# An encoder step on one core: plain tiles in two single accumulation banks, up inputs scaled once, memory keys moved ahead

## The chip, the core and the metric

One core of a Trainium2 chip runs one layer of an encoder. The metric is the device time of one execution, in microseconds (us). The engines of the core are called TensorE (PE, matmuls), VectorE (DVE), ScalarE (ACT), GpSimd (POOL) and SyncE (SP, which here issues DMAs).

## What is computed

```python
# x: 512 prompt + 64 sample tokens, D_MODEL = 1024; mem: 256 tokens; all float32
x += MixerBlock(RMSNorm(x))      # gated DeltaNet || gated linear attention, sigmoid-gated merge,
                                 # then the output projection (wo)
x += MemCrossAttn(RMSNorm(x), mem)   # 4 heads of 256: mq, mk, mv, softmax, mo
x += ConvFFN(RMSNorm(x))         # up (2 x 2816), causal conv of width 3, SiLU gate, down
y = RMSNorm(x)                   # outputs: y, the memory keys and values, and the new states
```

## The kernel before

Activations lie with features on partitions, eight tiles of 128, and tokens along the free axis: 576 columns, which the FFN pads to 580. Every float32 operand is split into a high and a low part (tiles with names in h and l, such as `xh` and `xl`, `oh` and `ol`, `ach` and `acl`), and a product is three matmuls: high weight by high and by low, low weight by high. Each runs as two matmuls over the columns, 256 and 320, or 290 and 290 in the FFN. So a *plain tile* (128 output features, eight tiles of input) is 48 matmuls. Where two output tiles share inputs, `products` (L1523) and `up_product` (L1953) work a pair with seven products of sums instead of eight: 84 matmuls for 96. These sums of weights (`ws`) and of activations (`ce`, `co`, `tu`, `tw`, `sh`, `sl`, `sw`) are made by VectorE, ScalarE and GpSimd.

PE accumulates in eight banks: `big` (L500) hands out two tiles of two banks each, `sm` (L503) four single banks. Plain tiles take `big`; products, norms, the attention and the recurrences take `sm`. A tile is emptied (evacuated) into SBUF in two pieces, 512 prompt and 64 sample columns (`pv`, `two`), before its buffer goes on. Weights come as raw tiles (`wr`), from which ScalarE casts the high half and VectorE subtracts the low half, or by DMAs that add into a tile (`w<-wt`, `w<-ws`); nine weight tiles exist. `fetch` (L638) brings weights ahead as far as tiles are free and `wlimit` allows.

The program's order is not written out. A `Driver` (L225) keeps a clock of its own for each engine: it walks the main chain, which yields time as it places matmuls, and lets spawned chains (`c_...` functions) place their work when their inputs are ready by its cost model. `V`, `A`, `G` name VectorE, ScalarE, GpSimd; `X` picks whichever ends sooner; `together` places several instructions as one piece, back to back. Because every instruction is written by one helper, the profile gives all of them line L257, and tiles tell them apart.

The stages that the change touches, in order:
- *Output tiles* (`out_tile`, L1754), eight rows m of two plain tiles each (one per branch), multiplied into the gates `gt` by VectorE. After rows 0 to 3 stand the gates' products, whose operands a chain makes from gate row 2 on (`GT0`).
- *The list* `ATT` (L115): the order of memory keys (`mk`), memory values (`mv`), the output projection (`wo`, by products, over the stored input `x`) and the queries (`mq`), one step per head. `c_norm` makes the queries' inputs behind `wo`.
- *Memory output* (`mo`): tiles 0 and 1 are plain and wait for the last head, and are ended by `mo_last` (L1915); tiles 2 to 7 are products (`MPAIRS`). Tile 0 is ended ahead of the products, tile 1 after. As each x tile ends, `c_mo` (L1860) adds its square to `acc` and makes the up inputs `xh` (ScalarE, x by gain, 512 and 64 columns) and `xl` (VectorE); `c_sums` (L1879) adds them back to `ce` and `co` and makes the sums of the FFN's products from them.
- *The up loop* (L2057): up tiles 0 to JS - 1, each in a pair j and 22 + j, are plain; the first takes its inputs in the order 0, 2, 3, 4, 5, 6, 7, 1. `up_evac` (L1945) multiplies the tile by the norm's broadcast `rbc`, so the first pair waits for the norm n3. The other pairs are products.
- *The down projection*: three parts as plain tiles (`dn1`, L2075) between the products, the rest by products.

Of the kernel before, what the change touches and what calls it, by code (L numbers as in the profile page):

```python
# [30 lines left out]
WF = 3  # L31
RF = 1
NGDN = 2
GT0 = 2
HOP = 0.2
BACK = 6.0
MARGIN = 0.6
# [74 lines left out]

WPAIRS = [(("wo", m), ("wo", m + 1)) for m in range(0, 8, 2)]

ATT = [("mk", 0), ("mv", 0), ("wo", 0), ("mv", 1), ("mk", 1), ("mq", 0), ("mq", 1), ("mk", 2), ("mq", 2), ("mk", 3), ("mq", 3)]  # L115
MPAIRS = [(("mo", m), ("mo", m + 1)) for m in range(2, 8, 2)]
JS = 5
AFTER = {8: 2, 9: 2, 10: 2, 11: 2, 14: 2, 15: 2, 16: 2, 17: 2, 20: 2, 21: 2}


# [338 lines left out]
def tile_trunk(ctx, tc, xT, memT, wt, wd, vec, cst, w0, wgate, st_gdn, st_conv, st_gla, st_ffn, ckT, cv,  # L459
# [43 lines left out]
    def sm():  # L503
        return drv.rotate("sm", 4, pq.tile([P, 512], F32, tag="sm", name=nm("sm")))

    def r4(ap, b=128):
        return ap.rearrange("p (a b) -> p a b", b=b)

# [61 lines left out]
    def emit_product(pair, prod):  # L570

        def dram(tile_):
            kind, idx = tile_
            if kind != "dn":
                return wt[WIDX[tile_]], 512
            m, p = idx
            n = len(PARTS[p]) * 64
            return wd[m, :, PART0[p] * 128:PART0[p] * 128 + 2 * n], n

        n = dram(pair[0])[1]  # L580
        if prod == "P1":
            r = halves_of[pair] = []
            for t_ in pair:
                raw = raw_tile()
                src, _ = dram(t_)
                DMA(raw[:, :2 * n], src)
                r += [(raw[:, 0:n], src[:, 0:n]), (raw[:, n:2 * n], src[:, n:2 * n])]
        r = halves_of[pair]
        (a11, d11), (a12, d12), (a21, _), (a22, d22) = r[:4]

        def total(a, b):
            s_ = slot("ws")
            V.tensor_tensor(s_[:, 0:n], a, b, op=ALU.add)
# [151 lines left out]
    def two(t_, o1=0, o2=TP):  # L745
        return r4(t_[:, o1:o1 + TP], 256), t_[:, o2:o2 + TS]

    def tile_proj(kind, idx, xs, box, order=None, w=T):
        wh, wl = weight(kind, idx)
        ps = big()  # L750
        box.append(ps)
        yield from proj(ps, wh, wl, xs, late=kind in SUMMED, order=order, w=w)

# [808 lines left out]
    def main():  # L1562
# [191 lines left out]
        def out_tile(m):  # L1754
            wh, wl = weight("out", m)
            gs = [gates.pop((kd, m)) for kd in ("gta", "gtb")]
            for a in range(2):
                ps = big()
# [58 lines left out]
        for kd, i in ATT:  # L1817
# [10 lines left out]
            else:  # L1828
# [20 lines left out]
        acc = slot("acc")  # L1849
        out = []  # L1850
        yield tuple(("att", hd) for hd in range(3))
        part = []
        for m in range(2):
# [5 lines left out]
        yield (("att", 3),)  # L1859
        def c_mo(m):  # L1860
            yield [x[m]]
            sq_acc(acc, x[m], m == 0)
            h, lo = slot("xh", F32R), slot("xl", F32R)
            g = vcol(C_GFFN + m)
            for t_ in (h, lo):
                G.memset(pads(f(t_)), 0.0)
# [3 lines left out]
            out.append((m, (h, lo)))  # L1870
            drv.done.add(("mo", m))
            fx[m] = h, lo
            if m ^ 1 in fx:
                drv.spawn(c_sums(m // 2))

# [2 lines left out]

        def c_sums(k):  # L1879

            (eh, el), (oh_, ol_) = fx[2 * k], fx[2 * k + 1]
            ce, co = slot("ce"), slot("co")
# [32 lines left out]
        def mo_last(m):  # L1915
            ps, wh, wl = part[m]
            yield from proj(ps, wh, wl, xs_of(ao[6:8]), False, True, k0=6)
            for xx, i in zip(two(x[m]), pv(ps)):
                V.tensor_tensor(xx, i, xx, op=ALU.add)
# [9 lines left out]
        wlimit[0] = len(WORDER)  # L1929
        out = [p for _, p in sorted(out, key=lambda t: t[0])]  # L1930
        xs = xs_of(out, 580)
# [12 lines left out]

        def up_evac(col, ps):  # L1945
            u = up_tile()
            V.tensor_tensor(r4(u[:, 2:582], 290), ps[:, :, 0:290], r4(N["rbc"][:, 0:580], 290), op=ALU.mult)
            states(col, u)
            return u

        ubanks, fus = {}, {}
# [105 lines left out]
        for kd, i in FFN[:-1]:  # L2057
            if kd == "up":
                j = i
                ba_, bb_ = [], []  # L2060
                yield from tile_proj("up", j, xs, ba_, (0, 2, 3, 4, 5, 6, 7, 1) if j == 0 else None, 580)
                if j == 0:
                    yield from tile_proj("up", NJ, xs, bb_, None, 580)
                    yield ("n3",)
                    use_norm("n3")
                drv.spawn(c_gate(j, up_evac(j, ba_[0])), 1)
                if j > 0:
                    yield from tile_proj("up", NJ + j, xs, bb_, None, 580)
# [6 lines left out]
            elif kd == "dn1":  # L2075
                m, p = i
                yield tuple(("act", j) for j in PARTS[p])
                wh, wl = weight("dn", i)
                ps = big()
                yield from proj(ps, wh, wl, act_of(p), late=True)  # L2080
                for xx, i_ in zip(two(x[m]), pv(ps)):
                    V.tensor_tensor(xx, xx, i_, op=ALU.add)
                if m == 7:
                    for k in PARTK[p]:
                        del full[k]
# [296 lines left out]
```

## Time and profile before

| | us |
|---|---|
| median of 3 runs | 1115.37 (1115.36 to 1116.72) |
| the profiled execution | 1116.34 |
| its span | 1114.6 |
| PE busy | 1092.0 |
| VectorE, ScalarE, GpSimd busy | 744.1, 692.8, 316.1 |

All times are counted from the start of the span. "Busy" is the time in which an engine works on an instruction; of PE it says nothing on the clock, which the throttle can halve: the profile has the granted clock as a column of its own, 1.00 being full speed. In a row of waits, `PE big L257 <- DVE gt` says that PE, about to write a tile `big`, was released by VectorE's instruction that writes `gt`. In a timeline row stand start, length, engine, operation, output and inputs, shape and count, and in brackets the idle time before it with what ended it. The DMA share is that of the sixteen DMA engines.

### The profile page before, as it was taken

How to read it: one execution, taken by the hardware profiler on the slowest of the kernel's cores; microseconds unless marked ns; L12 is line 12 of the kernel's file. 1: busy time of each engine (PE TensorE's matmuls, PEld its weight loads, DVE VectorE, ACT ScalarE, POOL GpSimd, SP SyncE). 2: the span in 40 equal slices, each digit the busy share in tenths (PEclk: the TensorE clock that was granted, in tenths of full speed). 3: DMA queues.
4: the chain of work that ended last, by engine and by line, in shares of the span. 5: the costliest groups of instructions: out<-in, count | busy, mean ns of one | idle time of the engine just before them, and what ended most of it. 6: DMA issues, size and time to landing. Idle time of an engine off the chain costs nothing. (4 is left out here: it accounts for less than half of the span.)

```text
span 1114.6 us, 21435 instructions
## 1 busy us (share of the span) xinstructions
PE 1092.0 (98%) x8227; PEld 1053.9 (95%) x8227; DVE 744.1 (67%) x1466; ACT 692.8 (62%) x1360; POOL 316.1 (28%) x549
## 2 busy tenths in 40 slices
PE   9999999999999999998999999999999999999997
PEld 8999989998988999898999999899999999999996
DVE  5666854864654866876557579657776777577665
ACT  6666646563754577475647666665875785668644
POOL 0344215230432222131210124223432333334321
PEclk9999999999999999999999999899999999999999
DMA  8666532454455779596764737775887887788744
GB/s 284 135 161 144 116 74 78 81 116 111 124 108 120 175 175 229 162 273 180 191 177 110 188 71 167 189 170 111 176 178 163 188 185 172 157 200 184 169 99 117
DMA packets 66598, 173.04 MB, mean 155 GB/s; under 512 B 7744, under 2 KB 14016, under 8 KB 66496
## 3 DMA queue, kind: packets, MB, share of 16 engines
q0 software_dynamic: 29808, 72.89, 38.1%
q1 hardware_dynamic: 36400, 98.26, 27.1%
q8 instruction: 65, 1.06, 0.4%
q10 hardware_dynamic: 288, 0.52, 0.1%
q14 instruction: 37, 0.30, 0.1%
HBM read 158.94 MB, written 5.37 MB: 147 GB/s over the span
## 5 line engine op out<-in xcount | busy, mean ns | idle before, releaser
L257 PE MATMUL big<-xh,w 128*128 128x256 f32 (+1 forms) x1728 | 322.3, 304 | 3.3 <-ACT xh L257 2.2
L257 PEld LDWEIGHTS big<-xh,w 128*128 128x128 f32 x1728 | 261.2, 191 | 8.7 <-POOL xl L257 2.4
L257 POOL DMA_DIRECT2D w<-wt x146 | 129.4, 893 | 364.8 <-ACT w L257 281.6
L257 PE MATMUL big<-xl,w 128*128 128x256 f32 (+1 forms) x864 | 185.9, 297 | 0.0
L257 ACT CAST w<-wr 128x512 fp32r<-128x512 f32 (+3 forms) x200 | 158.6, 796 | 23.2 <-PE big L257 17.3
L257 ACT ACTIVATE w<-wr 128x512 fp32r<-128x512 f32 (+3 forms) x179 | 142.5, 798 | 28.7 <-PE big L257 7.5
L257 PEld LDWEIGHTS big<-xl,w 128*128 128x128 f32 x864 | 144.8, 190 | 0.2 <-DVE xl L257 0.2
L257 PE MATMUL sm<-xh,w 128*128 128x290 f32 (+1 forms) x640 | 137.6, 297 | 0.3 <-DMA w<-wt 0.3
L257 PE MATMUL sm<-ach,w 128*128 128x288 f32 (+2 forms) x576 | 119.9, 299 | 6.0 <-DVE x L257 2.7
L257 PE MATMUL big<-ach,w 128*128 128x256 f32 (+1 forms) x672 | 119.6, 295 | 0.5 <-ACT ach L257 0.5
L257 PEld LDWEIGHTS sm<-xh,w 128*128 128x128 f32 x640 | 106.3, 189 | 0.5 <-DMA w<-wt 0.5
L257 PEld LDWEIGHTS big<-ach,w 128*128 128x128 f32 x672 | 101.7, 188 | 0.8 <-ACT ach L257 0.7
L257 PEld LDWEIGHTS sm<-ach,w 128*128 128x128 f32 x576 | 94.7, 190 | 7.6 <-DMA w<-ws 2.3
L257 ACT CAST w<-ws 128x512 fp32r<-128x512 f32 (+1 forms) x120 | 70.7, 602 | 33.9 <-DVE ws L257 17.3
L257 PE MATMUL sm<-xl,w 128*128 128x290 f32 (+1 forms) x320 | 87.9, 296 | 0.0
L257 PE MATMUL sm<-acl,w 128*128 128x288 f32 (+2 forms) x288 | 79.5, 297 | 0.0
L257 DVE SCALAR_TENSOR_TENSOR fc<-fu,vec,fc 128x578 f32<-128x578 f32 x88 | 71.3, 825 | 8.3 <-ACT fc L257 7.8
L257 PE MATMUL big<-acl,w 128*128 128x256 f32 x336 | 71.9, 295 | 0.3 <-DVE acl L257 0.3
L257 DVE TENSOR_TENSOR w<-ws,w 128x512 fp32r<-128x512 f32 (+1 forms) x91 | 61.2, 682 | 8.3 <-ACT w L257 6.6
L257 PEld LDWEIGHTS sm<-xl,w 128*128 128x128 f32 x320 | 60.5, 189 | 0.0
L257 PE MATMUL sm<-sh,w 128*128 128x290 f32 x272 | 57.8, 298 | 1.0 <-DMA w<-ws 1.0
L257 PEld LDWEIGHTS big<-acl,w 128*128 128x128 f32 x336 | 56.2, 188 | 0.5 <-DVE acl L257 0.5
(390 smaller groups left out, 2190.0 us busy)
## 6 DMA issues: line engine op xcount, KB each, us to landing
wr<-wt SPq DMA_DIRECT2D x134, 512.0 KB, 5.7
w<-wt POOLq DMA_DIRECT2D x62, 512.0 KB, 7.1
w<-wt POOLq DMA_DIRECT2D x84, 256.0 KB, 6.1
wr<-wd SPq DMA_DIRECT2D x24, 384.0 KB, 6.7
w<-wd POOLq DMA_DIRECT2D x24, 384.0 KB, 6.9
w<-ws POOLq DMA_DIRECT2D x28, 256.0 KB, 5.9
x<-xT SPq DMA_DIRECT2D x16, 288.0 KB, 5.6
mem<-memT SPq DMA_DIRECT2D x8, 256.0 KB, 4.8
```

Source lines behind the costliest of these rows:

```text
L257: fn(*args, **kw)
```

## The change

A plain tile of the output rows, the up loop and `dn1` now takes either a two-bank tile or a pair of single banks (`wide`): the single ones if two of the four come free over 0.3 us earlier, on the Driver's clock. Its evacuation follows the banks (256 and 320 columns, or 512 and 64), both pieces placed as one. Memory keys 1 and 2 stand ahead of the output projection. `c_mo` scales x once into `cx` (ScalarE, two instructions placed as one), casts `cx` to `xh` (ScalarE, 580 columns) and subtracts for `xl` (VectorE), and `c_sums` uses `cx` itself. The first up tile takes its inputs in the order 2, 3, 4, 5, 0, 6 (high weight by high and low), the low weight by the same six, and then 7 and 1, with a wait of its own for each input; the first up pair is copied out by ScalarE as it is and scaled later. The norm n3 is started by a chain of its own. One weight more may be fetched before the memory output ends, and the gate operands start one gate row later. One more up pair goes by products. The sums of weights of `wo` and `mo` go to VectorE or GpSimd, whichever ends sooner.

```diff
-GT0 = 2
+GT0 = 3
-ATT = [("mk", 0), ("mv", 0), ("wo", 0), ("mv", 1), ("mk", 1), ("mq", 0), ("mq", 1), ("mk", 2), ("mq", 2), ("mk", 3), ("mq", 3)]
+ATT = [("mk", 0), ("mv", 0), ("mk", 1), ("mk", 2), ("wo", 0), ("mv", 1), ("mq", 0), ("mq", 1), ("mq", 2), ("mk", 3), ("mq", 3)]
-JS = 5
+JS = 4
+    def wide():
+        q = sorted(max([0.0] + list(drv.wrote.get(n, {}).values()) + list(drv.seen.get(n, {}).values())) if n not in drv.fresh else float("inf")
+                   for n in drv.ring["sm"])
+        if len(q) == 4 and q[1] + 0.3 < drv.free_at("big")[0]:
+            return Pair(sm(), sm())
+        return big()
...
         def total(a, b):
-            V.tensor_tensor(s_[:, 0:n], a, b, op=ALU.add)
+            (X if pair[0][0] in ("wo", "mo") else V).tensor_tensor(s_[:, 0:n], a, b, op=ALU.add)
...
         def out_tile(m):
-                ps = big()
+                ps = wide()
-                for g, i in zip(two(gs[a]), pv(ps)):
-                    V.scalar_tensor_tensor(g, g, 1.0, i, op0=ALU.add, op1=ALU.mult)
+                V.together([("scalar_tensor_tensor", (g, g, 1.0, i), dict(op0=ALU.add, op1=ALU.mult)) for i, g in pieces(ps, gs[a])])
...
         def c_mo(m):
-            for a, b, n in ((0, 0, TP), (TP + 2, TP, TS)):
-                A.activation(h[:, a:a + n], x[m][:, b:b + n], AF.Identity, scale=g)
-                V.scalar_tensor_tensor(lo[:, a:a + n], x[m][:, b:b + n], g, f(h[:, a:a + n]), op0=ALU.mult, op1=ALU.subtract)
+            A.together([("activation", (c_[:, a], x[m][:, b], AF.Identity), dict(scale=g))
+                        for a, b in ((slice(0, TP), slice(0, TP)), (slice(TP + 2, TP + 2 + TS), slice(TP, T)))])
+            parts2(h[:, 0:580], lo[:, 0:580], c_[:, 0:580])
...
         def c_sums(k):
-            for c_, (h, lo) in ((ce, (eh, el)), (co, (oh_, ol_))):
-                X.tensor_tensor(c_[:, 0:580], f(h)[:, 0:580], f(lo)[:, 0:580], op=ALU.add)
+            (eh, el, ce), (oh_, ol_, co) = fx[2 * k], fx[2 * k + 1]
...
-        wlimit[0] = WORDER.index(("up", 0)) + 1
+        wlimit[0] = WORDER.index(("up", 0)) + 2
-        yield tuple(("mo", m) for m in range(8))
-        drv.spawn(c_rstat("n3", [(acc, 0)], 4, True, 2.0, None, TP + 2))
+        def first_up(ps):
+            wh, wl = weight("up", 0)
+            outs = [(ps[:, 0, 0:290], U1), (ps[:, 1, 0:290], U2)]
+            for ks in ((2, 3, 4, 5, 0, 6), (7, 1)):
+                for k in ks:
+                    yield (("mo", k),)
+                    h, lo, _ = fx[k]
+                    for o, c in outs:
+                        PE.matmul(o, wh[:, k * 128:k * 128 + 128], h[:, c], start=k == 2, stop=False)
+                    for o, c in outs:
+                        PE.matmul(o, wh[:, k * 128:k * 128 + 128], lo[:, c], start=False, stop=False)
+                    yield 0.7
+                for k in ks:
+                    for o, c in outs:
+                        PE.matmul(o, wl[:, k * 128:k * 128 + 128], fx[k][0][:, c], start=False, stop=k == 1)
+                    yield 0.4
+            wlimit[0] = len(WORDER)
...
+        def raw_evac(ps):
+            u = up_tile()
+            A.together([("copy", (u[:, 2 + c:292 + c], ps[:, i, 0:290]), {}) for i, c in ((0, 0), (1, 290))])
+            return u
...
                 if j == 0:
-                    yield from tile_proj("up", NJ, xs, bb_, None, 580)
+                    yield from tile_proj("up", NJ, xs, bb_, None, 580, wide)
+                    u0, u1 = raw_evac(ba_[0]), raw_evac(bb_[0])
                     yield ("n3",)
```

The change moves instructions. First VectorE, at output rows 6 and 7 before: `big_5535` and `big_5576` are row 6's tiles, `gt_5105` and `gt_5106` its gates, the 1024-column rows the low halves of weights of memory key 0.

```order
L257 SCALAR_TENSOR_TENSOR gt_5105<-gt_5105,big_5535 128x64
L257 TENSOR_TENSOR w_5453<-wr_5451,w_5452 128x1024
L257 SCALAR_TENSOR_TENSOR gt_5106<-gt_5106,big_5576 128x64
L257 TENSOR_TENSOR w_5534<-wr_5532,w_5533 128x1024
L257 SCALAR_TENSOR_TENSOR gt_5105<-gt_5105,big_5535 128x512
L257 SCALAR_TENSOR_TENSOR ml_5587<-mem_5378,vec,mh_5586 128x256 x2
L257 SCALAR_TENSOR_TENSOR tw_5575<-tu_5574,gt_4854 128x288
L257 SCALAR_TENSOR_TENSOR ml_5605<-mem_5379,vec,mh_5604 128x256 x2
L257 SCALAR_TENSOR_TENSOR gt_5106<-gt_5106,big_5576 128x512
```

The same place now, where row 6 is in `big_5544` and `big_5586`, and row 7's first tile in `sm_5625` and `sm_5626`:

```order
L257 TENSOR_TENSOR w_5457<-wr_5455,w_5456 128x1024
L257 TENSOR_TENSOR w_5543<-wr_5541,w_5542 128x1024
L257 SCALAR_TENSOR_TENSOR ml_5585<-mem_5382,vec,mh_5584 128x256
L257 SCALAR_TENSOR_TENSOR gt_5113<-gt_5113,big_5544 128x512
L257 SCALAR_TENSOR_TENSOR gt_5113<-gt_5113,big_5544 128x64
L257 TENSOR_TENSOR tu_5594<-gt_4973,gt_4857 128x288
...
L257 SCALAR_TENSOR_TENSOR gt_5114<-gt_5114,big_5586 128x512
L257 SCALAR_TENSOR_TENSOR gt_5114<-gt_5114,big_5586 128x64
...
L257 SCALAR_TENSOR_TENSOR gt_5246<-gt_5246,sm_5625 128x256
L257 SCALAR_TENSOR_TENSOR gt_5246<-gt_5246,sm_5626 128x320
```

The two pieces of a tile stand together, and row 7 no longer uses the two-bank tiles. Second ScalarE, at the end of the memory output before; `x_5780` is tile 1, the last, and the 1024-column rows are casts of up weights:

```order
L257 ACTIVATE sq_8470<-x_5780 128x576
L257 ACTIVATE xh_8471<-x_5780,vec 128x512
L257 ACTIVATE w_8476<-wr_8474 128x1024
L257 CAST w_8475<-wr_8474 128x1024
L257 ACTIVATE w_8479<-wr_8477 128x1024
L257 ACTIVATE xh_8471<-x_5780,vec 128x64
L257 CAST w_8478<-wr_8477 128x1024
```

And now, with `x_5767` as tile 1:

```order
L257 ACTIVATE sq_8527<-x_5767 128x576
L257 ACTIVATE cx_8530<-x_5767,vec 128x512
L257 ACTIVATE cx_8530<-x_5767,vec 128x64
L257 CAST xh_8528<-cx_8530 128x580
L257 CAST sh_8563<-tu_8510 128x580
L257 CAST sw_8581<-tw_8511 128x290
L257 ACTIVATE w_8590<-wr_8588 128x1024
```

The input's rows stand together ahead of the weights. Third VectorE at the same place before, from the evacuation of tile 1 on:

```order
L257 TENSOR_TENSOR x_5780<-big_7837,x_5780 128x512
L257 TENSOR_TENSOR x_5780<-big_7837,x_5780 128x64
L257 SCALAR_TENSOR_TENSOR xl_8466<-x_6181,vec,xh_8465 128x512
L257 SCALAR_TENSOR_TENSOR xl_8466<-x_6181,vec,xh_8465 128x64
L257 TENSOR_TENSOR ce_8467<-xh_8439,xl_8440 128x580
L257 TENSOR_TENSOR co_8468<-xh_8465,xl_8466 128x580
L257 SCALAR_TENSOR_TENSOR tw_8434<-tw_8434,co_8390 128x290
L257 TENSOR_TENSOR sw_8469<-tw_8434,sw_8469 128x290
L257 TENSOR_TENSOR acc_7726<-acc_7726,sq_8470 128x576
L257 SCALAR_TENSOR_TENSOR xl_8472<-x_5780,vec,xh_8471 128x512
```

And now, to the low half of tile 1 (`xl_8529`):

```order
L257 TENSOR_TENSOR x_5767<-big_7850,x_5767 128x512
L257 TENSOR_TENSOR x_5767<-big_7850,x_5767 128x64
L257 TENSOR_TENSOR xl_8456<-cx_8457,xh_8455 128x580
L257 TENSOR_TENSOR sw_8473<-tw_8413,sw_8473 128x290
L257 TENSOR_TENSOR tu_8510<-cx_8457,cx_8444 128x290
L257 TENSOR_TENSOR acc_7753<-acc_7753,sq_8527 128x576
L257 SCALAR_TENSOR_TENSOR tw_8511<-tu_8510,cx_8444 128x290
L257 TENSOR_TENSOR xl_8529<-cx_8530,xh_8528 128x580
```

The two sums `ce` and `co` are gone, and the low halves are one row each.

More of the change, by code (lines that the diff above doesn't have):

```diff
@@ L504, in sm, with __init__, __getitem__, pieces @@
         return drv.rotate("sm", 4, pq.tile([P, 512], F32, tag="sm", name=nm("sm")))
+    class Pair:
+        def __init__(self, *banks):
+            self.banks = banks
+        def __getitem__(self, key):
+            a, i, c = key
+            return self.banks[i][a, c]
+    def wide():
[4 more added lines that the diff above has]
+        return big()
+    def pieces(ps, *ts):
+        if isinstance(ps, Pair):
+            return list(zip((ps[:, 0, 0:256], ps[:, 1, 0:320]), *((t_[:, 0:256], t_[:, 256:T]) for t_ in ts)))
+        return list(zip(pv(ps), *(two(t_) for t_ in ts)))
     def r4(ap, b=128):
@@ L746, in two, with tile_proj @@
         return r4(t_[:, o1:o1 + TP], 256), t_[:, o2:o2 + TS]
-    def tile_proj(kind, idx, xs, box, order=None, w=T):
+    def tile_proj(kind, idx, xs, box, order=None, w=T, bank=None):
         wh, wl = weight(kind, idx)
-        ps = big()
+        ps = (bank or big)()
         box.append(ps)
@@ L1848, in main @@
                 drv.spawn(c_att(i))
-        acc = slot("acc")
-        out = []
+        facc = slot("acc")
         yield tuple(("att", hd) for hd in range(3))
@@ L1917, in mo_last @@
             yield from proj(ps, wh, wl, xs_of(ao[6:8]), False, True, k0=6)
-            for xx, i in zip(two(x[m]), pv(ps)):
-                V.tensor_tensor(xx, i, xx, op=ALU.add)
+            V.together([("tensor_tensor", (xx, i, xx), dict(op=ALU.add)) for xx, i in zip(two(x[m]), pv(ps))])
             drv.spawn(c_mo(m))
         yield from mo_last(0)
-        wlimit[0] = WORDER.index(("up", 0)) + 1
+        wlimit[0] = WORDER.index(("up", 0)) + 2
         yield from products(MPAIRS, [mops[hd] for hd in range(4)], mo_finish, (("mops", 3),))
@@ L1927, in main, with c_n3 @@
         drop(*part[1][1:])
-        yield tuple(("mo", m) for m in range(8))
-        wlimit[0] = len(WORDER)
-        out = [p for _, p in sorted(out, key=lambda t: t[0])]
-        xs = xs_of(out, 580)
-        drv.spawn(c_rstat("n3", [(acc, 0)], 4, True, 2.0, None, TP + 2))
-        CW = 578
+        CW = 578
+        def c_n3():
+            while not drv.ready(*(("mo", m) for m in range(8))):
+                yield WAIT
+            drv.spawn(c_rstat("n3", [(facc, 0)], 4, True, 2.0, None, TP + 2))
+        drv.spawn(c_n3())
+        def first_up(ps):
[15 more added lines that the diff above has]
+            wlimit[0] = len(WORDER)
         def states(col, u):
@@ L1946, in up_evac @@
             u = up_tile()
-            V.tensor_tensor(r4(u[:, 2:582], 290), ps[:, :, 0:290], r4(N["rbc"][:, 0:580], 290), op=ALU.mult)
+            if isinstance(ps, Pair):
+                V.together([("tensor_tensor", (u[:, 2 + c:292 + c], ps[:, i, 0:290], N["rbc"][:, c:c + 290]), dict(op=ALU.mult)) for i, c in ((0, 0), (1, 290))])
+            else:
+                V.tensor_tensor(r4(u[:, 2:582], 290), ps[:, :, 0:290], r4(N["rbc"][:, 0:580], 290), op=ALU.mult)
             states(col, u)
+            return u
+        def raw_evac(ps):
+            u = up_tile()
+            A.together([("copy", (u[:, 2 + c:292 + c], ps[:, i, 0:290]), {}) for i, c in ((0, 0), (1, 290))])
             return u
@@ L2060, in main @@
                 ba_, bb_ = [], []
[L2061 removed]
                 if j == 0:
[L2063 removed]
+                    ba_.append(wide())
+                    yield from first_up(ba_[0])
+                    xs = [(fx[k][0][:, 0:580], fx[k][1][:, 0:580]) for k in range(8)]
+                else:
+                    yield from tile_proj("up", j, xs, ba_, None, 580, wide)
+                if j == 0:
+                    yield from tile_proj("up", NJ, xs, bb_, None, 580, wide)
+                    u0, u1 = raw_evac(ba_[0]), raw_evac(bb_[0])
                     yield ("n3",)
                     use_norm("n3")
+                    drv.spawn(c_gate(j, u0, True), 1)
+                    drv.spawn(c_act(j, u1, True), 1)
+                    continue
                 drv.spawn(c_gate(j, up_evac(j, ba_[0])), 1)
                 if j > 0:
[L2068 removed]
+                    yield from tile_proj("up", NJ + j, xs, bb_, None, 580, wide)
                 if j == JS - 1:
@@ L2078, in main @@
                 wh, wl = weight("dn", i)
-                ps = big()
+                ps = wide()
                 yield from proj(ps, wh, wl, act_of(p), late=True)
-                for xx, i_ in zip(two(x[m]), pv(ps)):
-                    V.tensor_tensor(xx, xx, i_, op=ALU.add)
+                V.together([("tensor_tensor", (xx, xx, i_), dict(op=ALU.add)) for i_, xx in pieces(ps, x[m])])
                 if m == 7:
```

12 lines of the change are left out of this document (4 added, 8 removed).

## The prediction

> **What bounds the kernel now.** I read the page's first lines, then the table of waits of TensorE (PE), then windows of the span, and last the timelines at the places where PE stood still.
>
> ```profile
> span 1114.6 us, 21435 instructions
> PE 1092.0 (98%) x8227; PEld 1053.9 (95%) x8227; DVE 744.1 (67%) x1466; ACT 692.8 (62%) x1360; POOL 316.1 (28%) x549
> PE big L257 <- ACT xh L257: 2.2, 1, 2.2
> PE big L257 <- DVE gt L257: 2.1, 1, 2.1
> PE sm L257 <- DMA w<-ws: 3.0, 2, 2.1
> PE sm L257 <- ACT xh L257: 1.0, 1, 1.0
> PE big L257 <- DVE fu L257: 0.6, 1, 0.6
> ```
>
> PE is busy 98% of the span: the time is the number of matmuls by their pace, plus a few stalls, plus what follows them. Each row gives what PE wanted and what released it, the total in us, the times and the longest. Three waits are over 2 us: for an operand (ACT xh), for banks that VectorE empties (DVE gt), for a weight (DMA w<-ws). The next table, of windows (PE busy time and count, PEld, DVE, ACT, POOL, granted clock, DMA share, GB/s), shows each of the three with what comes behind it.
>
> ```profile
> 450.00:454.00 4.00, 1.86 (x14) 1.66 (x13) 2.98 (x6) 1.62 (x2) 1.84 (x1) 1.00 0.54 174
> 454.00:457.40 3.40, 3.40 (x17) 3.40 (x16) 3.37 (x7) 0.00 (x0) 0.00 (x0) 0.50 0.70 277
> 501.00:505.00 4.00, 1.94 (x15) 1.70 (x14) 0.54 (x2) 1.25 (x3) 1.14 (x2) 1.00 1.07 334
> 505.00:508.60 3.60, 3.60 (x18) 3.60 (x17) 1.43 (x3) 0.68 (x1) 0.00 (x0) 0.53 0.67 131
> 693.70:697.40 3.70, 3.70 (x30) 3.70 (x29) 3.70 (x8) 3.70 (x7) 1.48 (x1) 1.00 0.00 0
> 697.40:699.80 2.40, 0.36 (x3) 0.12 (x1) 2.40 (x5) 2.40 (x5) 1.04 (x3) 0.99 0.26 22
> 699.80:706.60 6.80, 6.68 (x29) 6.68 (x30) 6.08 (x16) 4.40 (x6) 3.87 (x5) 0.50 0.97 230
> 706.60:713.30 6.70, 6.70 (x50) 6.34 (x49) 2.82 (x8) 2.38 (x4) 1.11 (x4) 1.00 1.04 271
> ```
>
> After each stall PE counts as fully busy but the granted clock is 0.50: a stretch of 3.4 us behind the first two, of 6.8 us behind the third. In the last row, at full clock, 50 matmuls take 6.70 us, 0.134 us each. At half clock they start 0.24 us apart:
>
> ```profile
> 505.63 0.45 PE L257 MATMUL sm<-ach,w 128*128 128x288 f32 x1
> 505.87 0.45 PE L257 MATMUL sm<-acl,w 128*128 128x288 f32 x1
> ```
>
> So a half-clock stretch of 3.4 us costs 3.4 x (1 - 0.134/0.24) = 1.5 us, and a stall of 2.1 us that is followed by one costs 3.6 in all.
>
> The Trainium skill ("TensorE: Matmul & The Clock Gate", part 1, "What's actually happening") has the throttle come back after an idle window of about 3.4 us. By that rule none of these stalls, 2.1 to 2.2 us long, would cost more than its own length and the sum below would be about 1.5 us poorer at the output tiles. The rows decide: the clock is at 0.50 behind each.
>
> **The change part by part.**
>
> *One more up pair by products.* JS goes from 5 to 4: 96 plain matmuls become 84. 12 x 0.134 = **-1.6 us**, on PE's own path, and nothing hides it. The extra sums for the weights lie on engines that are busy 28 to 67% of the span.
>
> *Output tiles.* The timeline of VectorE around the stall at 451.2:
>
> ```profile
> 448.85 1.71 DVE L257 TENSOR_TENSOR w<-wr,w 128x1024 fp32r<-128x1024 f32 x1
> 451.58 0.22 DVE L257 SCALAR_TENSOR_TENSOR gt<-gt,big 128x64 f32<-128x64 f32 x1 [1.02 <-PE big L257]
> 451.72 1.22 DVE L257 TENSOR_TENSOR w<-wr,w 128x1024 fp32r<-128x1024 f32 x1
> 452.85 0.68 DVE L257 SCALAR_TENSOR_TENSOR gt<-gt,big 128x512 f32<-128x512 f32 x1
> ```
>
> A tile's 64-column piece ran, then a 1024-column weight subtraction, and only then the 512-column piece of the tile before, which frees the bank pair that PE needs. After the change the pieces go out together, and the two tiles of output row 7 sit in single banks that were freed during row 5; the next two-bank tile is one row later, 48 matmuls or 6.4 us. The subtractions still stand ahead of row 6's evacuation, but up to 6.4 us of PE work now covers 1.2 to 1.7 us of them. The stall goes with its half clock: 2.1 + 1.5 = **-3.6 us**. Next late there is the weight for row 7 itself, which was there when PE resumed.
>
> *Up inputs scaled once.* In before, each of the eight up inputs costs VectorE two lo pieces and one sum of the halves:
>
> ```profile
> L257 DVE SCALAR_TENSOR_TENSOR xl<-x,vec,xh 128x512 fp32r<-128x512 f32 x8 | 6.6, 823 | 0.0
> L257 DVE SCALAR_TENSOR_TENSOR xl<-x,vec,xh 128x64 fp32r<-128x64 f32 x8 | 2.2, 277 | 0.0
> L257 DVE TENSOR_TENSOR co<-xh,xl 128x580 f32<-128x580 f32 x4 | 3.0, 751 | 0.0
> L257 DVE TENSOR_TENSOR ce<-xh,xl 128x580 f32<-128x580 f32 x4 | 3.0, 751 | 0.0
> L257 ACT CAST sh<-tu 128x580 fp32r<-128x580 f32 x4 | 2.7, 672 | 0.8 <-DVE tu L257 0.8
> 660.00:693.70 33.70, 32.04 (x240) 31.60 (x240) 30.40 (x62) 23.38 (x44) 12.93 (x24) 1.00 0.83 196
> ```
>
> That is 6.6 + 2.2 + 3.0 + 3.0 = 14.8 us; after, eight subtractions at the 0.75 of the sums, 6.0 us. VectorE gives up 8.8 us of work. ScalarE gains one 580-column cast per input, 8 x 0.67 = 5.4 us. In the last row, the memory-output stage, VectorE was busy 30.4 of 33.7 us and ScalarE 23.4: some 24 and 28 after, so neither is full. The two stalls of the stage are waits for banks that VectorE empties late:
>
> ```profile
> 689.25 0.75 DVE L257 TENSOR_TENSOR co<-xh,xl 128x580 f32<-128x580 f32 x1
> 689.92 0.81 DVE L257 TENSOR_TENSOR x<-x,sm 128x288 f32<-128x288 f32 x2
> 690.41 0.40 PE L257 MATMUL sm<-ach,w 128*128 128x288 f32 x1 [0.62 <-DVE x L257]
> ```
>
> The evacuation at 689.92 stood right behind a sum that goes. This 0.6 and the 1.0 of the same kind five us earlier (the ACT xh row of the waits on sm) are **-1.6 us**; bounds 0 and -1.6, and I take the full end because such sums are the very rows ahead of the evacuation. One up weight more is fetched ahead in this stage: two casts of 1.04 us (rows below), in ScalarE's free 6 us.
>
> *First up tile.* It began at 693.7 (first row x30) and the next began at 706.7: 13.0 us for 48 matmuls and ten one-column sums, which at full clock are 48 x 0.134 = 6.4 and about 0.9. So 5.7 us are lost. ScalarE's timeline:
>
> ```profile
> 695.40 0.69 ACT L257 ACTIVATE sq<-x 128x576 f32<-128x576 f32 x1
> 695.99 0.71 ACT L257 ACTIVATE xh<-x,vec 128x512 fp32r<-128x512 f32 x1
> 696.60 1.04 ACT L257 ACTIVATE w<-wr 128x1024 fp32r<-128x1024 f32 x1
> 697.55 1.03 ACT L257 CAST w<-wr 128x1024 fp32r<-128x1024 f32 x1
> 698.49 1.05 ACT L257 ACTIVATE w<-wr 128x1024 fp32r<-128x1024 f32 x1
> 699.44 0.33 ACT L257 ACTIVATE xh<-x,vec 128x64 fp32r<-128x64 f32 x1
> ```
>
> The last input's 64-column piece waited 2.8 us behind three weight casts. After, its two pieces and the cast stand together ahead of those weights, the tile takes k=1 last of the hi and lo passes, and 36 matmuls of the six early inputs and 4 of k=7 (5.4 us) precede it. On ScalarE from x being ready: 0.69 + 0.71 + 0.33 + 0.67 = 2.4 us, on VectorE evacuation 0.81 and lo 0.75: 4.0. The order puts another lo, a sum of squares and three 290-column sums between the two on VectorE: two at 0.75 and three at half of that, 2.6 more. So between nothing and 4.0 + 2.6 - 5.4 = 1.2 us is late, and the evacuation itself can stand behind one more such row, 0.75. I take 1.4, near the end where the queue is full, since these rows are ahead in the order. Left lost 1.4 of 5.7: **-4.3 us**; bounds -2.0 (the stall stays over 2 us and takes one half-clock stretch) and -5.7.
>
> *Raw evacuation of the first pair.* PE's 0.6 (big <- DVE fu) waits for a norm that VectorE multiplies in; ScalarE now copies the banks without it: **-0.6 us**. The scaling, two VectorE passes of 0.76, is moved behind; there VectorE was busy 2.8 of 6.7 us.
>
> *Memory keys forward.* The tiles of memory keys 1 and 2 come ahead of the attention input's output projection (wo). Nothing is added, but the key-1 tile no longer stands between values 1 and the first queries. The rows there:
>
> ```profile
> 528.34 0.63 PE L257 MATMUL big<-w,mh 128*128 128x512 f32 x2
> 534.75 0.81 DVE L257 SCALAR_TENSOR_TENSOR xl<-x,vec,xh 128x576 fp32r<-128x576 f32 x1
> 540.66 0.28 PE L257 MATMUL big<-mh,w 128*128 128x256 f32 x1
> 546.32 0.96 PE L257 MATMUL sm<-dg,onesr 128*128 128x512 f32 x4
> ```
>
> Values 1 run from 528.3 to 540.7, key 1 to 546.3. The queries' last operand is there at 535.6, so 5.1 us of slack remain when the 5.7 us of key 1 are gone; only the norm's broadcast (546.3) has to come as early as before. Zero. For everything else that moves (two-bank tiles of the down projection in single banks, other bank orders, the fetch of one weight more) I add **+1.0** for small new waits: two of the size of the 0.6-us rows above; bounds 0 and +3, one more wait of 2.1 us without a half clock.
>
> The skill's same page ("A second HAM failure mode: psum-queue depth-cycling") speaks against the change: a kernel that cycles its accumulation banks idles in small gaps and the throttle comes and goes. By it every plain tile moved to the single banks could bring half-clock stretches. The trace disagrees: products cycle through these four banks all through 660 to 693.7, and the clock there is 1.00.
>
> **Sum.** -1.6 - 3.6 - 1.6 - 4.3 - 0.6 + 1.0 = -10.7 us. The profiled execution took 1116.34 us (span 1114.6 and 1.7 around it), so 1105.6; it was 1.0 above the median 1115.37, and so 1104.7 against the runs.
>
> **Rivals.** The 501-us stall goes too: two more key tiles, 11.4 us of PE work, run ahead of the output projection, and the DMA queues get that time to fetch. For it: the DMA share of 1.07 in that row says that the engines were full, so that any transfer done earlier helps. Against: weights are fetched only as their nine buffers come free, so time ahead of the stage is not lead in it. It gives 2.1 + 1.5 more, 1101.1. The stretch of half clock stays at the first up tile: its stall is 2.2 us or more, because x of k=1 is emptied behind a full VectorE queue. Then -2.0 for -4.3 and 1107.0. The banks were not what PE waited for, or single banks aren't chosen: only the products and the ScalarE edits count, -1.6 - 1.6 and part of the up tile, about 1111. On the other side: the queries start 5.7 us sooner after the output projection, and the softmax of heads 0 to 2 now has no key tile between. If the norm is later than values 1, PE waits for up to the 5.7 us of cover that was taken, with a half-clock stretch or two (1.5 to 3.0), and the same again before the third queries, where key 2 and its 5.7 us used to stand: 2 x 7.2 = 14.4 against 10.7, so 1119. It decides once the operands are over 5.1 us later than in before's rows, and needs both places; a wait at one place alone leaves 1112.
>
> **How the numbers follow.** Forecast 0.50, stall at 501 gone 0.18, half clock at the up tile 0.17, banks not the cause or one query wait 0.08, both query waits 0.07. Likeliest: 1104.7. Low 1099: the 501 stall gone (1101.1), no new waits (-1.0) and the up tile whole (-1.4) make 1098.7. High 1111: the half clock stays and new waits are 3 (1109), or the third rival. A measurement of this kernel tells about 0.2%, 2.2 us, from no change. Faster 0.88, same 0.05, slower 0.07.
>
> **What would show it.** Right: no half-clock stretch behind the output tiles or the first up tile; the rows of the waits on DVE gt, ACT xh and DVE fu gone; no ce and co sums from xh and xl on VectorE; 12 matmuls fewer. Wrong: a wait of PE over 2 us at the first queries, at the first up tile or in a place that had none, or a clock under 1.00 in a window that had 1.00.

## The result, and the profile after

The changed kernel takes 1107.86 us (median of 4, 1107.23 to 1109.66) against 1115.58 (median of 4) for the one before: 7.7 us less, a ratio of 0.9931 with a 95% interval from 0.9914 to 0.9949. The forecast was 1104.7 within 1099 to 1111. The profiled execution took 1107.82 us, its span is 1106.1, 8.5 below that of before.

The profile's first lines, and the first six rows of what TensorE (PE) waited for in the changed kernel:

```profile
span 1106.1 us, 21400 instructions
PE 1087.6 (98%) x8215; PEld 1049.5 (95%) x8215; DVE 746.8 (68%) x1466; ACT 700.5 (63%) x1383; POOL 313.6 (28%) x539
PE sm L257 <- DMA w<-ws: 2.6, 2, 2.4
PE sm L257 <- DVE x L257: 1.8, 4, 0.7
PE sm L257 <- DMA w<-wt: 1.6, 1, 1.6
PE sm L257 <- ACT fu L257: 1.3, 2, 0.7
PE warm L257 <- POOL onesr L257: 1.0, 1, 1.0
PE big L257 <- ACT xh L257: 1.0, 1, 1.0
```

PE's matmuls are 12 fewer (8215 for 8227). The wait for DVE gt is gone, that for DVE fu too, ACT xh is 1.0 for 2.2. The weight wait on `w<-ws` stayed, and there is one that was not there, 1.6 us on `w<-wt`. The windows of the same places (columns as in the prediction):

```profile
450.00:454.00 4.00, 4.00 (x32) 4.00 (x32) 4.00 (x9) 1.85 (x2) 0.00 (x0) 1.00 0.96 332
498.00:502.00 4.00, 1.62 (x13) 1.39 (x12) 0.28 (x1) 2.62 (x5) 1.73 (x2) 1.00 1.05 363
502.00:506.00 4.00, 4.00 (x21) 4.00 (x20) 1.93 (x4) 1.46 (x3) 0.53 (x1) 0.57 1.08 293
695.40:699.00 3.60, 2.46 (x17) 1.98 (x15) 3.60 (x9) 3.26 (x7) 0.00 (x0) 1.00 0.36 100
699.00:702.40 3.40, 3.29 (x19) 3.27 (x20) 2.94 (x8) 3.40 (x5) 2.19 (x2) 0.70 0.20 24
702.40:705.80 3.40, 3.40 (x23) 3.40 (x22) 2.20 (x7) 3.40 (x6) 3.40 (x7) 0.80 0.70 190
```

At the output tiles (first row) PE runs through. In the output projection the wait and the half clock behind it are as before. The first up tile still has one stretch of half clock (0.70 and 0.80 are the two windows that it straddles), though its waits are now 1.0 and 0.3 us:

```profile
691.77 0.43 PE L257 MATMUL big<-xh,w 128*128 128x290 f32 x2
698.31 0.54 PE L257 MATMUL big<-xh,w 128*128 128x290 f32 x2 [0.98 <-ACT xh L257]
699.11 0.54 PE L257 MATMUL big<-xl,w 128*128 128x290 f32 x2 [0.26 <-DVE xl L257]
699.48 1.25 PE L257 MATMUL sm<-keep,acc 128*128 128x1 f32 x10
...
701.79 0.69 PE L257 MATMUL sm<-xh,w 128*128 128x290 f32 x2
```

The tile begins at 691.77 and the next, in single banks, at 701.79: 10.0 us for 13.0. The two halves of its last input are still 1.2 us late (0.98 for `xh`, 0.26 for `xl`).

The new wait is early in the memory output. GpSimd's rows there, then ScalarE's, then PE's:

```profile
656.03 1.75 POOL L257 TENSOR_TENSOR ws<-wr,wr 128x512 f32<-128x512 f32 x1
657.73 0.85 POOL L257 DMA_DIRECT2D w<-wt  x1
...
663.44 0.86 POOL L257 DMA_DIRECT2D w<-wt  x1 [0.70 <-ACT w L257]
```

```profile
657.81 0.62 ACT L257 CAST w<-ws 128x512 fp32r<-128x512 f32 x1 [1.65 <-POOL ws L257]
```

```profile
670.07 0.93 PE L257 MATMUL sm<-ach,w 128*128 128x288 f32 x5 [1.62 <-DMA w<-wt]
```

A sum of two weights runs on GpSimd in 1.75 us, ScalarE stands 1.65 us for it, and the DMAs that add a weight's low half, issued behind ScalarE's casts, are late for PE. Of the 124 sums of weights (tiles `ws`) in this kernel, it is the only one that GpSimd makes.

### The profile page after: what moved, and what is told of

The parts are those of the page before. It is cut to its first block, busy times and chain, and to the rows that moved or that the text cites. A ratio compares the mean times of both kernels' runs of the same rounds, so it can differ in the third digit from the quotient of the medians.

```text
span 1106.1 us, 21400 instructions
## 1 busy us (share of the span) xinstructions
PE 1087.6 (98%) x8215; PEld 1049.5 (95%) x8215; DVE 746.8 (68%) x1466; ACT 700.5 (63%) x1383; POOL 313.6 (28%) x539
## 5 line engine op out<-in xcount | busy, mean ns | idle before, releaser
L257 PE MATMUL big<-xh,w 128*128 128x256 f32 (+2 forms) x1568 | 293.0, 304 | 1.6 <-ACT xh L257 1.0
L257 PEld LDWEIGHTS big<-xh,w 128*128 128x128 f32 x1568 | 235.9, 190 | 6.9 <-issue 2.0
L257 PE MATMUL big<-xl,w 128*128 128x256 f32 (+2 forms) x784 | 168.4, 296 | 0.3 <-DVE xl L257 0.3
L257 PE MATMUL sm<-xh,w 128*128 128x290 f32 (+1 forms) x768 | 162.0, 298 | 0.6 <-ACT fu L257 0.5
L257 PEld LDWEIGHTS big<-xl,w 128*128 128x128 f32 x784 | 131.7, 189 | 0.7 <-DVE xl L257 0.7
L257 PEld LDWEIGHTS sm<-xh,w 128*128 128x128 f32 x768 | 126.3, 189 | 1.1 <-ACT fu L257 1.1
L257 PE MATMUL big<-ach,w 128*128 128x256 f32 x624 | 111.4, 295 | 0.5 <-ACT ach L257 0.5
L257 PE MATMUL sm<-xl,w 128*128 128x290 f32 (+1 forms) x384 | 103.1, 297 | 0.0
L257 PE MATMUL big<-acl,w 128*128 128x256 f32 (+1 forms) x312 | 66.7, 295 | 0.3 <-DVE acl L257 0.3
L257 PEld LDWEIGHTS sm<-acl,w 128*128 128x128 f32 x312 | 59.0, 191 | 0.0
```

The source lines that it names most:

```text
L257: fn(*args, **kw)
```

## The experiments

Times are compared by the ratio to the kernel before, run on the same chip; the interval of each ratio is about 0.2% to either side. The changed kernel's ratio is 0.9931 [0.9914, 0.9949]. For us below, a ratio is multiplied by 1115. Both ratios of a comparison have such an interval, so a difference under about 0.0025, or 2.8 us, is not clear of the noise; below that, the traces are what speaks, one execution of each kernel.

**No single banks.** `wide` always returns a two-bank tile.

```diff
-        if len(q) == 4 and q[1] + 0.3 < drv.free_at("big")[0]:
-            return Pair(sm(), sm())
```

> Every plain tile takes a two-bank tile again; the rest of the change stays (pieces back to back, scaled inputs, first tile, order). Theory: the single banks themselves removed the wait at the output tiles, so a wait of about 2.1 us and a half-clock stretch of 1.5 us come back at output row 7: 3.6 us slower than the changed kernel, about 1111.5. Rival: placing the two pieces together was enough, and the banks add nothing: within 0.5 us of the changed kernel. If the waits at the end of the FFN (3.1 us before, 1.1 after) come back here, they belong to the banks too.

1114.98 us (1111.12 to 1117.18), 0.9994 [0.9979, 1.0009]: 7.0 us slower than the changed kernel. But the wait at the output tiles did not come back:

```profile
PE big L257 <- DVE gt L257: 0.4, 1, 0.4
```

The theory named the wrong place. Waits came in the output projection (for weights, 1.9 us before the matmul at 499 and 1.5 before that at 504, and 1.2 for VectorE's x before that at 537) and in the FFN. PE's waits of this kernel from 780 on:

```profile
PE sm L257 <- ACT fu L257: 1.4, 3, 0.5
PE sm L257 <- DVE x L257: 0.9, 1, 0.9
PE sm L257 <- DMA w<-wd: 0.7, 1, 0.7
PE sm L257 <- DMA w<-wt: 0.5, 1, 0.5
PE sm L257 <- ACT sq L257: 0.4, 1, 0.4
```

In the changed kernel the same stretch has only these:

```profile
PE sm L257 <- ACT fu L257: 0.5, 1, 0.5
PE sm L257 <- DVE x L257: 0.2, 1, 0.2
```

The profiled execution was among the faster ones (1111.93), so its waits don't explain the whole median. What the 7.0 us are made of stays in part open: the run with the up tiles alone, below, has 2.5 of them.

**Output tiles as before**, in two-bank tiles and with the pieces placed apart; the rest of the change stays.

```diff
-                ps = wide()
+                ps = big()
-                V.together([("scalar_tensor_tensor", (g, g, 1.0, i), dict(op0=ALU.add, op1=ALU.mult)) for i, g in pieces(ps, gs[a])])
+                for g, i in zip(two(gs[a]), pv(ps)):
+                    V.scalar_tensor_tensor(g, g, 1.0, i, op0=ALU.add, op1=ALU.mult)
```

> Only the output tiles go back: a two-bank tile each, emptied in two pieces placed apart. Theory after the run without single banks, where the wait at the output tiles was 0.56 us: the pieces apart bring the wait of about 2 us at row 7 back, with a half-clock stretch in some executions; 2 to 3.6 us slower than the changed kernel, 1110 to 1111.5. Rival: the wait stays under 0.6 us, because the gate operands' later start or another part of the change removed it; then within 0.5 us.

1112.69 us (1110.94 to 1116.23), 0.9985 [0.9972, 0.9998]: 6.0 us slower, more than expected, and more than the wait below and a stretch of half clock (3.0 + 1.5 us). The wait, and VectorE's timeline at it:

```profile
PE big L257 <- DVE gt L257: 3.0, 1, 3.0
```

```profile
449.72 0.21 DVE L257 SCALAR_TENSOR_TENSOR gt<-gt,big 128x64 f32<-128x64 f32 x1
449.85 1.22 DVE L257 TENSOR_TENSOR w<-wr,w 128x1024 fp32r<-128x1024 f32 x1
452.59 0.22 DVE L257 SCALAR_TENSOR_TENSOR gt<-gt,big 128x64 f32<-128x64 f32 x1 [1.52 <-PE big L257]
452.73 2.13 DVE L257 TENSOR_TENSOR w<-wr,w 128x1024 fp32r<-128x1024 f32 x1
454.78 0.68 DVE L257 SCALAR_TENSOR_TENSOR gt<-gt,big 128x512 f32<-128x512 f32 x1
```

Between the 64-column piece of the tile whose banks PE wants (449.72) and its 512-column piece (454.78) stand two weight subtractions and the other tile's small piece, which itself waits for PE. Both this kernel and the one above have two-bank tiles at the output rows. With the pieces together the wait is 0.4 us, with subtractions between them 3.0. So the order on VectorE is enough to bring the wait or to take it away, and single banks give 0.4 us more at most. Whether single banks would also have removed it with the pieces apart was not run.

**Plain down tiles in two-bank tiles**, and **plain up tiles in two-bank tiles**, one at a time.

```diff
-                ps = wide()
+                ps = big()
                 yield from proj(ps, wh, wl, act_of(p), late=True)
```

> Only the plain tiles of the down projection take two-bank tiles again; in the changed kernel two of 24 stand in single banks. Theory: the up tiles' single banks are what cleared the FFN's end, so this run is within 1 us of the changed kernel. Rival: the down tiles hold up the products behind them; 2 to 4 us slower, with waits for VectorE's x and for weights at the end of the FFN.

1105.31 us (1102.85 to 1109.15), 0.9921 [0.9895, 0.9946], overlapping the changed kernel's. The list of PE's waits is the changed kernel's within 0.3 us: the two down tiles show no effect.

```diff
-                    yield from tile_proj("up", j, xs, ba_, None, 580, wide)
+                    yield from tile_proj("up", j, xs, ba_, None, 580)
```

and likewise for the other tile of each pair and for the first.

> Only the plain up tiles take two-bank tiles again; in the changed kernel four or five of eight stand in pairs of single banks. Theory: they are what made the run without single banks 7 us slower, by 4.3 us of waits in and at the end of the FFN: 3 to 5 us slower than the changed kernel, with waits of single-bank products on ScalarE's evacuations after 790. Rival: the up tiles' banks don't matter, the slow run owed its time to the output tiles' banks and what they shift in the output projection: within 1 us.

1109.50 us (1109.37 to 1110.32), 0.9953 [0.9939, 0.9968]: 2.5 us slower, at the edge of the noise. Its waits from 780 on are those of the kernel without single banks, but for the weights':

```profile
PE sm L257 <- ACT fu L257: 1.4, 3, 0.5
PE sm L257 <- DVE x L257: 1.1, 1, 1.1
PE sm L257 <- ACT sq L257: 0.4, 1, 0.4
```

These are 2.2 us more than in the changed kernel (2.9 for 0.7), about the measured difference, and they stand up to 390 us behind the tiles themselves. How the up tiles' banks act so far behind was not taken apart, so that they cause these waits is likely and not shown.

**JS at 5 again.**

```diff
-JS = 4
+JS = 5
```

> JS is 5 again: one pair of up tiles plain instead of by products, 12 matmuls more. Theory: 12 x 0.134 = 1.6 us slower than the changed kernel, about 1109.5, and nothing else moves. Rival: the 2.2 us that the end of the FFN gained without a forecast come from JS, because it shifts which bank and which weight stand where from there on: then 3.8 us slower, about 1111.7.

1109.22 us (1108.10 to 1111.84), 0.9949 [0.9930, 0.9969]: 2.0 us slower, within the noise and between the two. Both were there in part: waits of 0.5, 0.5, 0.6 and 1.2 us before the matmuls at 896, 991, 1000 and 1086 (in the changed kernel, 0.5 and 0.2 us from 780 on), but also no half clock up to the kernel's end in the profiled execution. Its windows at the output projection:

```profile
498.00:502.00 4.00, 1.35 (x11) 1.12 (x10) 0.38 (x1) 2.72 (x5) 1.72 (x2) 1.00 1.06 351
502.00:506.00 4.00, 4.00 (x32) 4.00 (x32) 2.43 (x5) 1.95 (x4) 0.86 (x1) 1.00 1.08 307
```

PE idles longer here than in the changed kernel (1.35 us busy of 4 for 1.62), and the clock behind is 1.00 where that had 0.57. A wait of this size gets its half-clock stretch in one execution and not in another.

**The keys where they stood.**

```diff
-ATT = [("mk", 0), ("mv", 0), ("mk", 1), ("mk", 2), ("wo", 0), ("mv", 1), ("mq", 0), ("mq", 1), ("mq", 2), ("mk", 3), ("mq", 3)]
+ATT = [("mk", 0), ("mv", 0), ("wo", 0), ("mv", 1), ("mk", 1), ("mq", 0), ("mq", 1), ("mk", 2), ("mq", 2), ("mk", 3), ("mq", 3)]
```

> The memory keys stand where they stood before; the rest of the change stays. Theory: the order of the keys is worth nothing, within 1 us of the changed kernel; the weight wait in the output projection stays at 2.1 to 2.5 us with its half-clock stretch. Rival: the new waits of the memory output (0.7 and 1.8 us, at 661 and 668) come from the other order, which lets that stage begin before the last head is done: 2.0 to 2.5 us faster than the changed kernel, and the two waits are gone.

1108.72 us (1107.31 to 1110.17), 0.9942 [0.9924, 0.9959]: 1.2 us slower, which the noise covers: about the theory's nothing, but not as it had it. The weight wait at 498 is gone, and other waits stand at the head of the output projection. PE's waits from 470 to 545, and the windows:

```profile
PE sm L257 <- DVE x L257: 2.1, 2, 1.4
PE sm L257 <- ACT ach L257: 1.4, 1, 1.4
PE sm L257 <- DVE acl L257: 0.7, 1, 0.7
```

```profile
476.00:480.00 4.00, 1.89 (x13) 1.44 (x12) 3.73 (x6) 4.00 (x8) 0.14 (x1) 1.00 0.99 260
480.00:484.00 4.00, 2.56 (x13) 2.33 (x12) 3.93 (x8) 2.78 (x6) 2.24 (x3) 0.58 1.00 301
```

The projection's operands are made by ScalarE and VectorE after the last output tile. With the wait at the output tiles gone, PE arrives there before they are ready; the two keys in between cover that. The new waits of the memory output (0.5 and 2.0 us) stayed, against the rival.

**The up inputs made as before**, with sums back to `ce` and `co`.

```diff
-            parts2(h[:, 0:580], lo[:, 0:580], c_[:, 0:580])
+            for a, b, n in ((0, 0, TP), (TP + 2, TP, TS)):
+                A.activation(h[:, a:a + n], x[m][:, b:b + n], AF.Identity, scale=g)
+                V.scalar_tensor_tensor(lo[:, a:a + n], x[m][:, b:b + n], g, f(h[:, a:a + n]), op0=ALU.mult, op1=ALU.subtract)
```

> The up inputs are made as before (two ScalarE pieces, two VectorE pieces, and sums back to ce and co); the rest stays. Theory: the bank waits late in the memory output come back (1.6 us), and the new early waits (0.7 and 1.8 us) stay, since they hang on sums of weights that GpSimd now makes: 1.5 us slower or a little more, as the first up tile loses some too. Rival: the early waits come from the casts that ScalarE does more; they go, and the run is 0.5 to 1 us faster than the changed kernel.

1108.89 us (1108.05 to 1109.36), 0.9941 [0.9923, 0.9958]: 1.1 us slower, which agrees with the theory's 1.5 but is within the noise. The early waits stayed (0.6 and 1.3 us) and late bank waits came back, 3.1 us of them:

```profile
684.94 0.37 PE L257 MATMUL sm<-ach,w 128*128 128x288 f32 x1 [0.79 <-DVE x L257]
690.60 0.40 PE L257 MATMUL sm<-ach,w 128*128 128x288 f32 x1 [2.27 <-DVE x L257]
```

**Sums of weights on VectorE alone.**

```diff
-            (X if pair[0][0] in ("wo", "mo") else V).tensor_tensor(s_[:, 0:n], a, b, op=ALU.add)
+            V.tensor_tensor(s_[:, 0:n], a, b, op=ALU.add)
```

> The sums of weights of the output projections are VectorE's alone again. Theory: the 1.75 us that the first such sum of the memory output takes on GpSimd holds ScalarE's casts and the weight DMA behind them; without it the wait of 1.6 us at 668 falls under 0.5 us and the run is about 1.5 us faster than the changed kernel, 1106.4. Rival: the wait stays, since the casts are late for the up inputs that ScalarE makes ahead of them: within 0.5 us.

1103.05 us (1102.83 to 1103.62), 0.9898 [0.9883, 0.9913]: 3.7 us faster than the changed kernel, over twice the theory's gain. The same sum on VectorE, and GpSimd's DMA that was late:

```profile
654.48 0.78 DVE L257 TENSOR_TENSOR ws<-wr,wr 128x512 f32<-128x512 f32 x1
```

```profile
659.82 0.86 POOL L257 DMA_DIRECT2D w<-wt  x1 [0.33 <-ACT w L257]
```

The sum takes 0.78 us for 1.75, the DMA is issued at 659.8 for 663.4, and both early waits are gone from the trace. At the first up tile the wait for ACT xh is 0.4 us for 1.0, and the clock behind it stayed whole. It also stayed whole behind the wait in the output projection (2.4 us), which is as long as in the changed kernel: that part of the gain can't be put down to the sum.

**The norm's sums later**, 16 matmuls into the second up tile.

```diff
-            while not drv.ready(*(("mo", m) for m in range(8))):
+            while not drv.ready("up0", *(("mo", m) for m in range(8))):
...
+                    for n_, y_ in enumerate(tile_proj("up", NJ, xs, bb_, None, 580, wide)):
+                        if n_ == 3:
+                            drv.done.add("up0")
+                        yield y_
```

> The norm's ten one-column sums move from the end of the first up tile into the second, 16 matmuls later; the waits of the first tile stay. Theory: the clock is halved because the two waits (1.0 and 0.3 us) and the sums, 1.2 us in which hardly any column runs, fall in one stretch; apart, there is no half clock at 700 and the run is 1.5 us faster. Rival: the waits alone are enough, or the place of the stretch decides from run to run; the half clock comes in some executions and the median moves by under 0.7 us.

1104.70 us (1104.19 to 1105.76), 0.9913 [0.9898, 0.9928]: 2.0 us faster, within the noise. The windows from the first up tile's wait on:

```profile
694.00:697.40 3.40, 2.75 (x21) 2.52 (x19) 3.40 (x8) 2.98 (x7) 0.00 (x0) 1.00 0.52 140
697.40:700.80 3.40, 2.81 (x19) 2.57 (x20) 3.40 (x8) 3.40 (x6) 0.95 (x2) 1.00 0.02 5
700.80:704.20 3.40, 3.40 (x29) 3.37 (x28) 0.89 (x4) 3.40 (x5) 1.62 (x5) 1.00 0.82 147
```

The waits are as long as in the changed kernel, and the clock is whole here (there is one half-clock stretch in this execution, behind the 1.8 us wait of the memory output). That agrees with the theory, but does not show it: the kernel with JS at 5 had those waits and the sums behind them, and a whole clock too in its profiled execution. Nor do the medians show it: in this execution the wait in the output projection is split (1.4 and 1.0 us) and has no half clock behind it either, so the 2.0 us can have come from there.

**Both of the last two**, then with **JS at 3**, then with **one weight made otherwise**.

> Two edits together: the sums of weights on VectorE alone, and the norm's column sums 16 matmuls later. Theory: they remove different waits (3.7 and 2.0 us apart), but each also took the half-clock stretch at the first up tile away, which can go only once: 4.0 to 4.5 us faster than the changed kernel, a ratio to before of about 0.989. Rival: they add up to 5.7 us, 0.988 or less.

1102.46 us (1100.60 to 1103.50), 0.9889 [0.9870, 0.9907]: 4.7 us faster than the changed kernel, nearer to the theory's 4.0 to 4.5 than to the rival's 5.7, which the interval does not exclude.

```diff
-JS = 4
+JS = 3
```

> The kernel of the two edits with JS at 3: one more up pair by products, 12 matmuls fewer. Theory: the pair again gives 12 x 0.134 = 1.6 us. Rival: the products begin before the norm and the sums of the inputs are ready, and waits of over 1.6 us at their start (there is one of 0.9 to 1.6 us now) take it back.

1100.95 us (1098.98 to 1101.39), 0.9872 [0.9857, 0.9887]: 1.5 to 1.9 us faster than the kernel of the two edits, as 12 matmuls fewer would give; the intervals overlap.

```diff
-        if prod in ("P1", "P2", "Q4") or prod == "Q5" and n > 256:
+        if prod in ("P1", "P2", "Q4") or prod == "Q5" and n > 256 and pair[0][0] != "wo":
```

> The kernel of the two edits, and in the output projection the low half of the product Q5's weight is a subtraction by VectorE or GpSimd instead of a DMA that adds. Theory: the wait of 2.4 us for that DMA at 498 goes with its half-clock stretch where there is one, 2 to 3 us faster than the kernel of the two edits. Rival: the DMA queues are full there (share 1.07), and another weight is as late: within 0.7 us.

1097.84 us (1097.36 to 1099.31), 0.9850 [0.9835, 0.9864]: 4.3 to 4.6 us faster than the kernel of the two edits (ScalarE's pass that prepared these DMAs goes with them), and the fastest of all, 16.3 below the kernel before on its chip (1114.15). The window of the wait, and all that PE still waits for from 470 to 545:

```profile
498.00:502.00 4.00, 4.00 (x33) 4.00 (x32) 3.10 (x6) 3.18 (x6) 1.10 (x2) 1.00 1.07 297
PE big L257 <- DVE kraw L257: 0.2, 1, 0.2
```

The DMA share is 1.07 (1.05 in the changed kernel), so the DMA engines stayed as full and PE no longer waits for them. More came than the one wait: the two on VectorE's x behind it, 1.1 us together, went too.

## Why the prediction was right, and where it was not

The time is inside the range, 3.2 us above the number. The profiled executions differ by 8.5 us, and the stretches of the span show where, against the -10.7 of the sum:

| stretch, from PE's first matmul of each | forecast | measured |
|---|---|---|
| start to output row 4 | 0 | +0.5 |
| output rows 4 to 7 | -3.6 | -4.3 |
| first memory key to first up tile | -1.6, and +1.0 for new waits anywhere | +1.9 |
| first up tile | -4.3 | -3.0 |
| second up tile to the end | -2.2 | -3.6 |

So the total is right in part by luck: gains that no step had, at the end, offset losses that no step had, in the middle. By its own steps:

- *One more up pair*, -1.6: right. The count fell by 12, and JS by one either way moved the time by 1.5 to 2.0 us, which agrees but is within the noise.
- *Output tiles*, -3.6: it measured -4.3, the stall with its half clock and a weight wait of 0.4 us besides, and it was wrong in half of its reason. From the start of row 4 to the first memory key it is 25.6 us (432.2 to 457.8) for 29.9 (431.7 to 461.6). The prediction gave the gain to the pieces and to the single banks alike; with the pieces together, the runs leave at most 0.4 us to the banks.
- *Up inputs scaled once*, -1.6: right. The two waits late in the memory output went, and the run with the old inputs has late waits on banks again.
- *First up tile*, -4.3: mis-sized, it measured -3.0. The lateness of 1.4 us was right (1.2), but a stretch of half clock came with it, which the prediction had tied to a stall over 2 us. No run put the old order of inputs back, so this size rests on the two traces.
- *Raw evacuation*, -0.6: the wait is gone from the trace; no run undid this part alone.
- *Memory keys forward*, 0: right as a sum only. The prediction looked for what the move takes away and found slack. The run with the old order shows that it also covers the output projection's operands, which the gain at the output tiles had laid bare.
- *New waits*, +1.0: this is the step that failed most. The memory output alone has two new ones, 0.6 and 1.6 us, and they hang on the edit that lets the sums of weights go to GpSimd: with the sums on VectorE both are gone, and the kernel is 3.7 us faster. The prediction listed other work that moved and gave this edit no price. On GpSimd the sum takes 1.75 us for 0.78, and ScalarE and the weight DMA behind it wait. The output projection's waits grew besides, from 3.1 to 3.7 us.
- *The FFN's end*, which no step had: the kernel before waits 2.5 us from 780 on (1.0 on DVE x, 1.0, 0.3 and 0.2 on weights), the changed one 0.7. The runs with the up tiles in two-bank tiles and with JS at 5 have more waits there again.

Of the signs that the prediction named for itself, two did not come: the half clock behind the first up tile stayed, and the wait for ACT xh shrank (1.0 for 2.2 us) and did not go.

Of the rivals, the half clock at the first up tile came nearest: it forecast 1107.0, and the profiled execution has that stretch. But it had tied the stretch to a stall of 2.2 us or more, and it came behind one of 1.2, so its number is near partly by luck. The wait at 501 stayed, and the full DMA queues were no reason for it by themselves: with the one weight made otherwise it went at the same DMA share. The rival on the other side, waits at the queries, did not show.

## What to carry to other kernels

When two instructions free one buffer, look at what can stand between them in the engine's order before giving the buffer more banks: here subtractions in between went with 3.0 us of waiting against 0.4. Price every edit that lets a scheduler choose an engine, even where it looks like a relief: what is queued behind the slower engine's instruction pays for it, here for a single one of 124. And a wait that goes makes PE arrive sooner at the next dependence; look there for what covers it.

## What the runs showed of the hardware

A stretch of half clock, 3.4 us long or (at the first up tile of the kernel before) 6.8, is not a fixed price of a wait. Waits of 2.3 to 2.6 us at the same place in the output projection were followed by it in the changed kernel (2.4 us) and not in the kernels with JS at 5 (2.6), with two-bank down tiles (2.3) and with the sums on VectorE (2.4). Two waits of 1.0 and 0.3 us with ten one-column matmuls behind them were followed by it in the changed kernel, and not in the one with JS at 5. That fits the Trainium skill ("TensorE: Matmul & The Clock Gate", part 1, "What's actually happening") in that the throttle's window runs freely, so that it matters where in it the idle time falls; it does not agree with an idle stretch of a whole window as the condition, since none of these was longer than 2.6 us. Single executions of one kernel differ too: the kernel without single banks ran from 1111.1 us, at a mean clock of 0.997, to 1117.2 us, at 0.994, though among its ten executions time and clock do not go strictly together.
